# Light experts of a mixture layer: f32 products side by side on raw weights instead of products with split weights

## The chip, the cores and the metric

The kernel runs on one core of one Trainium2 chip. The metric is the device time of one execution in microseconds (us), lower is better. PE is TensorE (products), DVE is VectorE, ACT is ScalarE, POOL is GpSimd, and SP is the engine whose queue issues the loads of weights.

## The reference

Two layers of a diffusion backbone, 256 latent and 256 context tokens of width 1024, all in f32. Each layer modulates a normed input, projects it, runs three kinds of attention (GQA, differential, MLA), projects back and adds a gated result. Layer 0 has a dense feed-forward network, layer 1 a mixture of eight experts with the two best per token. The change concerns the mixture alone:

```python
def _moe_swiglu(h, w_router, w_in, w_out):
    logits = (h @ w_router).astype(jnp.float32)
    top_val, top_idx = lax.top_k(logits, TOP_K)          # TOP_K = 2 of N_EXPERTS = 8
    top_w = jax.nn.softmax(top_val, axis=-1)
    gates = jnp.sum(jax.nn.one_hot(top_idx, N_EXPERTS) * top_w[..., None], axis=-2)
    out = jnp.zeros_like(h)
    for e in range(N_EXPERTS):
        out = out + gates[..., e:e + 1] * _swiglu(h, w_in[e], w_out[e])
    return out
```

where `_swiglu(h, w_in, w_out)` is `(silu(gate) * up) @ w_out` with gate and up the two halves of `h @ w_in`; `w_in[e]` is 1024 x 3584 and `w_out[e]` 1792 x 1024. The result is close to an f32 computation.

## The kernel before

**Split products.** A product of full f32 precision is made of products of the rounded type f32r. An operand is split into a high part (a cast to f32r, on ACT, line 90) and a low part (the f32 value minus the high part, on DVE, line 91). Then high x high, high x low and low x high are added in PSUM: three matmuls for one.

**The experts** (`experts`, from line 1112; the last stage of the kernel). The router counts the tokens of each expert and ranks the experts by that count. The four with most tokens are "heavy" (128 slots for tokens), the four with fewest "light" (64 slots, `LIGHT`). They are worked on in the order heavy 0, light 4, heavy 1, light 5, 2, 6, 3, 7 (`order`, line 1121); names carry that rank, so `gub040mm` is a bank of gate products of rank 4, half 0, and `gub041s` a bank of up products of rank 4, half 1. `gather` (line 1172) picks the tokens of an expert with a product by a 0/1 matrix, for two heavy experts or all four light ones at once. `up(e, half)` makes half of gate and up (896 columns each, in two banks `mm` and two banks `s`) over eight loads of 128 rows of `w_in`, applies silu and multiplies, and transposes the result (`ht`). `down(e, half)` multiplies it with four loads of `w_out` (three with two blocks of 128 rows, one with one) into the two banks `pv` and `mod`. After the second half the sum is scaled by the gate, split, and scattered back to the tokens with a product by the transposed 0/1 matrix. For each expert the code calls `up` half 0, `down` half 1 of the expert before it, `up` half 1, `down` half 0; a scheduler then fixes the order on each engine, and the engines keep to it.

**A load** (`load`, line 1089) takes the next raw buffer in turn and issues one transfer on SP, which waits in order for that buffer to come free. There are five raw buffers (four of `rawp`, one of `xp`). Each load is then split into `wh` and `wl` (four buffers of each, `XW_BUFS`), by one cast on ACT and one subtraction on DVE over the whole load; the raw buffer is free when the subtraction is done.

**A light expert before.** Its 64 tokens' high and low parts stand side by side in one stationary operand of 128 columns (`xlight`), so that one product with `wh` and one with `wl` do for all: two passes instead of three (line 1202). One load of `w_in` is 8 products of 448 columns (12 for a heavy expert), one block of `w_out` 4 products of 512 columns (6 for a heavy one). The two halves of partitions are added afterwards: per bank two copies on ACT, two additions on DVE, then silu and a multiplication (lines 1236 to 1241).

**Two products at once.** `matmul(..., tile_position=(0, 64 * i))` puts a stationary operand of 64 columns into columns 64 i and up of the array, and its result into partitions 64 i and up. The kernel before uses it in the attention, line 779, with f32 operands and 64 columns, alternating between both places:

```python
for k in range(nk):
    for hi in range(2):
        nc.tensor.matmul(acc[64 * hi:64 * hi + 64, 0:256], lhsT=vs[hi][k], rhs=both[hi][:, k],
                         start=(k == 0), stop=(k == nk - 1), tile_position=(0, 64 * hi))
```

Line 336 (`gate_rows`) is a single f32 product of 512 columns with the full width of the array.

Of the kernel before, what the change touches and what calls it, by code (L numbers as in the profile page):

```python
# [9 lines left out]
F32 = mybir.dt.float32  # L10
# [7 lines left out]
P = 128  # L18
# [9 lines left out]
NE = 8  # L28
# [51 lines left out]
class Net:  # L80
# [1014 lines left out]

    def weights_in(self, w, half, k, b, parts=False):
        src = w[0][:, :, k, :, 896 * half:896 * half + 896].rearrange("p e g f -> p (e g) f")
        raw = self.load([P, 2, 896], src, f"wi{b}{half}{k}")
# [11 lines left out]
    def experts(self, l, mp, xp, block, acc, resid, first):  # L1110
# [58 lines left out]
        def gather(e0):  # L1169
            dispatched = dispatch(e0)  # L1170
            ne = H if light[e0] else 2
            if light[e0]:
                tiles = [make() for make in self.lights]
            else:
                tiles = {(e, s): xp.tile([P, KC, P], F32R, tag=f"xe{s}", name=f"xe{b}{e}{s}", bufs=2)
                         for e in (e0, e0 + 1) for s in "hl"}
            for k0 in range(0, KC, 2):
                ps = self.ps.tile([P, 512], F32, tag="tr", name=f"ga{b}{e0}{k0}")
                tmp = xp.tile([P, 512], F32, tag="xtmp", name=f"xt{b}{e0}{k0}")
                for u in range(2):  # L1180
# [17 lines left out]
            for u in range(ne):  # L1198
                if light[e0]:
                    xe[e0 + u] = [tiles[k // 4][:, k % 4, u].rearrange("p a s -> p (a s)") for k in range(KC)]  # L1200
                else:
                    xe[e0 + u] = [(tiles[e0 + u, "h"][:, k], tiles[e0 + u, "l"][:, k]) for k in range(KC)]
# [9 lines left out]
        def up(e, half):  # L1212
            banks = [[self.ps.tile([P, 512], F32, tag=tag, name=f"gu{b}{e}{half}{tag}{j}") for j in range(2)] for tag in ("mm", "s")]
            w = weights(e)
            for k in range(KC):
                if first and e == half == 0 and k < XW_BUFS:
                    wh, wl = self.early.pop(k)
                else:
                    wh, wl = self.weights_in(w, half, k, f"{b}{e}")
                passes = products(xe[e][k], wh, wl)  # L1220
                for n, (lhs, rhs) in enumerate(passes):
                    for gu in range(2):
                        for j in range(2):
                            nc.tensor.matmul(banks[gu][j][:, 0:448], lhsT=lhs, rhs=rhs[:, gu, 448 * j:448 * j + 448],
                                             start=(k == n == 0), stop=(k == KC - 1 and n == len(passes) - 1))
            hn = xp.tile([P, 896], F32, tag="hn", name=f"hn{b}{e}{half}")
            if light[e]:
                nc.gpsimd.memset(hn[LIGHT:P], 0.0)  # L1228
            for j in range(2):
                o = hn[:, 448 * j:448 * j + 448]  # L1230
                if light[e]:

                    o = o[0:LIGHT]
                    u = xp.tile([P, 512], F32, tag="xtmp", name=f"u{b}{e}{half}{j}")[0:LIGHT, 0:448]
                    g2, u2 = banks[0][j], banks[1][j]
                    nc.scalar.copy(out=o, in_=g2[LIGHT:P, 0:448])
                    nc.vector.tensor_tensor(out=o, in0=o, in1=g2[0:LIGHT, 0:448], op=ALU.add)
                    nc.scalar.copy(out=u, in_=u2[LIGHT:P, 0:448])
                    nc.vector.tensor_tensor(out=u, in0=u, in1=u2[0:LIGHT, 0:448], op=ALU.add)
                    nc.scalar.activation(out=o, in_=o, func=AF.Silu)  # L1240
# [3 lines left out]
                nc.vector.tensor_tensor(out=o, in0=o, in1=banks[1][j][:, 0:448], op=ALU.mult)  # L1244
            hh = xp.tile([P, 7, P], F32R, tag="hth", name=f"hth{b}{e}{half}", bufs=2)
            hl = None if light[e] else xp.tile([P, 7, P], F32R, tag="htl", name=f"htl{b}{e}{half}", bufs=2)
            for f0, nf in ((0, 4), (4, 3)):
# [3 lines left out]
                pv = ps[:, 0:nf * P].rearrange("p (f s) -> p f s", s=P)  # L1251
                if light[e]:
                    self.split(pv[:, :, 0:LIGHT], hh[:, f0:f0 + nf, 0:LIGHT], hh[:, f0:f0 + nf, LIGHT:P])
                else:
                    self.split(pv, hh[:, f0:f0 + nf], hl[:, f0:f0 + nf])
            hts[e, half] = [hh[:, f] if light[e] else (hh[:, f], hl[:, f]) for f in range(7)]

        def down(e, half):
# [7 lines left out]
            for f0 in range(0, 7, 2):  # L1266
                nf = min(2, 7 - f0)
                raw = self.load([P, nf, D], w[:, :, 7 * half + f0:7 * half + f0 + nf].rearrange("p e f n -> p (e f) n"),
                                f"wo{b}{e}{half}{f0}")
                wh = self.xw.tile([P, nf, D], F32R, tag="wh", name=f"woh{b}{e}{half}{f0}")  # L1270
# [5 lines left out]
                todo = [(f, n, lhs, rhs) for f, h, lo in held for n, (lhs, rhs) in enumerate(products(ht[f], h, lo))]  # L1276
# [3 lines left out]
                final = (6, len(products(ht[6], None, None)) - 1)  # L1280
                for (f, n, lhs, rhs), o in turns:
                    nc.tensor.matmul(ys[e][o], lhsT=lhs, rhs=rhs[:, 512 * o:512 * o + 512],
                                     start=(half == 0 and f == 0 and n == 0), stop=(half == 1 and (f, n) == final))
# [6 lines left out]
            for o in range(2):  # L1290
                sl = slice(512 * o, 512 * o + 512)
                if last:
                    yg = xp.tile([P, 512], F32, tag=("xtmp", "hn")[o], name=f"yg{b}{e}{o}")
                    nc.vector.scalar_tensor_tensor(out=yg, in0=ys[e][o], scalar=gsl, in1=self.gate[:, sl], op0=ALU.mult, op1=ALU.mult)
# [415 lines left out]
```

## Time and profile before

| | |
|---|---|
| median of 3 runs | 1532.55 us (1532.23 to 1544.02) |
| profiled execution | 1529.3 us, of which its span 1527.4 us |
| PE busy | 1387.7 us, 91% of the span |
| DVE busy | 1204.0 us, 79% |
| ACT busy | 832.0 us, 54% |
| POOL busy | 214.8 us, 14% |
| bytes moved | 318.66 MB, mean 209 GB/s |

The span is the time from the first to the last instruction of the profiled execution. Busy time counts an instruction from its start to its end; matmuls overlap one another, so a timeline shows their distance better than their durations do. An engine's row in a table of waits says for whom it stood still. The granted clock is a share of TensorE's full rate.

### The profile page before, as it was taken

Reading aid. Unit: us, or ns where it says so; the run is one execution under the profiler, and the core shown is the slowest. Engines: PE = TensorE matmul, PEld = TensorE weight load, DVE = VectorE, ACT = ScalarE, POOL = GpSimd, SP = SyncE. Lnnn points to the kernel's source line nnn. Section 1 sums busy time; section 2 is a strip of 40 time slices with the busy share of each in tenths; the row PEclk is TensorE's granted clock in tenths of the full one; section 3 lists DMA queues with packets and bytes.
Section 4 is the critical chain, followed back from the end, with each engine's and each line's share of the span. In section 5 each row is a group of like instructions: output and inputs, shape, how many; then the busy total and the mean of one; then the engine's idle time right before and its main releaser. Section 6 shows DMA issues by size and latency. Waiting matters only on the chain. (4 is left out here: it accounts for less than half of the span.)

```text
span 1527.4 us, 21068 instructions
## 1 busy us (share of the span) xinstructions
PE 1387.7 (91%) x7750; PEld 1114.6 (73%) x7750; DVE 1204.0 (79%) x1960; ACT 832.0 (54%) x1213; POOL 214.8 (14%) x174
## 2 busy tenths in 40 slices
PE   5999999999999999989999898798899899889874
PEld 1876755777789998979878556687777678767652
DVE  4577588776888787785679776888988989898896
ACT  2444455776342222234446673577767767766753
POOL 1001011111413333320220013000000000000041
PEclk9999999999999999999999999799999989999997
DMA  9265354223754566535335101499999989999982
GB/s 352 79 227 174 135 197 166 83 83 112 251 184 141 171 234 206 195 109 186 97 112 180 49 1 60 148 310 318 318 347 366 348 293 335 356 335 336 371 281 99
DMA packets 133991, 318.66 MB, mean 209 GB/s; under 512 B 7814, under 2 KB 49888, under 8 KB 133880
## 3 DMA queue, kind: packets, MB, share of 16 engines
q1 hardware_dynamic: 130032, 311.69, 58.5%
q10 hardware_dynamic: 3720, 5.54, 1.1%
q8 instruction: 63, 1.03, 0.3%
q14 instruction: 48, 0.39, 0.1%
q0 software_dynamic: 128, 0.01, 0.0%
HBM read 316.16 MB, written 1.05 MB: 208 GB/s over the span
## 5 line engine op out<-in xcount | busy, mean ns | idle before, releaser
L91 DVE TENSOR_TENSOR wilb<-wib,wihb 128x1792 fp32r<-128x1792 f32 (+1 forms) x140 | 266.6, 1933 | 24.8 <-ACT wihb L90 24.7
L90 ACT CAST wihb<-wib 128x1792 fp32r<-128x1792 f32 (+1 forms) x140 | 215.8, 1566 | 62.4 <-DMA wib<-in_moe_w_in_dram 38.4
L118 PE MATMUL fp<-hhf,fwl 128*128 128x256 f32 x704 | 199.7, 284 | 1.0 <-DVE fwl L91 1.0
L116 PE MATMUL fp<-hhf,fwh 128*128 128x256 f32 x704 | 200.0, 284 | 0.0
L117 PE MATMUL fp<-hlf,fwh 128*128 128x256 f32 x704 | 199.9, 284 | 0.0
L851 POOL TENSOR_TENSOR x<-x,otf 128x512 f32<-128x512 f32 x68 | 110.9, 1656 | 281.4 <-DVE otf L850 266.6
L91 DVE TENSOR_TENSOR wolb<-wob,wohb 128x2048 fp32r<-128x2048 f32 x64 | 128.2, 2018 | 16.4 <-ACT wohb L90 14.9
L116 PEld LDWEIGHTS fp<-hhf,fwh 128*128 128x128 f32 x704 | 134.0, 190 | 4.3 <-issue 2.6
L117 PEld LDWEIGHTS fp<-hlf,fwh 128*128 128x128 f32 x704 | 134.2, 191 | 2.9 <-issue 1.5
L118 PEld LDWEIGHTS fp<-hhf,fwl 128*128 128x128 f32 x704 | 134.0, 190 | 2.9 <-DVE fwl L91 1.5
L90 ACT CAST fwh<-fi 128x1024 fp32r<-128x1024 f32 x64 | 66.2, 1050 | 102.0 <-PE yf L118 64.9
L90 ACT CAST wohb<-wob 128x2048 fp32r<-128x2048 f32 x64 | 107.3, 1694 | 23.5 <-DMA wob<-in_moe_w_out_dram 14.3
L91 DVE TENSOR_TENSOR fwl<-fi,fwh 128x1024 fp32r<-128x1024 f32 x64 | 88.8, 1396 | 36.5 <-ACT fwh L90 36.4
L738 ACT ACTIVATE p<-s,st 128x512 f32<-128x512 f32 (+1 forms) x120 | 73.8, 618 | 25.0 <-DVE st L733 20.0
L733 DVE TENSOR_REDUCE st<-s 128x1 f32<-128x512 f32 (+1 forms) x100 | 67.8, 685 | 17.9 <-PE s L118 15.3
L1228 POOL MEMSET hnb<- 64x896 f32 x8 | 6.7, 843 | 483.8 <-PE htb L1250 483.8
L273 DVE SCALAR_TENSOR_TENSOR macc<-wm,sc,macc 128x512 f32<-128x512 f32 x84 | 73.6, 887 | 0.4
L116 PE MATMUL yf<-foh,fhh 128*128 128x512 f32 x176 | 71.9, 408 | 0.0
L118 PE MATMUL yf<-foh,fhl 128*128 128x512 f32 x176 | 70.3, 401 | 0.0
L117 PE MATMUL yf<-fol,fhh 128*128 128x512 f32 x176 | 69.8, 397 | 0.0
L91 DVE TENSOR_TENSOR fol<-fo,foh 128x1024 fp32r<-128x1024 f32 x32 | 39.0, 1222 | 25.6 <-ACT foh L90 25.5
L90 ACT CAST foh<-fo 128x1024 fp32r<-128x1024 f32 x32 | 33.5, 1049 | 45.9 <-PE fp L117 43.1
(832 smaller groups left out, 3537.4 us busy)
## 6 DMA issues: line engine op xcount, KB each, us to landing
wib<-in_moe_w_in_dram SPq DMA_DIRECT2D x128, 896.0 KB, 6.7
wm<-in_w_mod_dram SPq DMA_DIRECT2D x48, 1024.0 KB, 5.3
wob<-in_moe_w_out_dram SPq DMA_DIRECT2D x48, 1024.0 KB, 7.8
fi<-in_ffn_w_in_dram SPq DMA_DIRECT2D x64, 512.0 KB, 5.0
fo<-in_ffn_w_out_dram SPq DMA_DIRECT2D x16, 1024.0 KB, 5.2
wi<-in_w_in_dram SPq DMA_DIRECT2D x15, 1024.0 KB, 6.1
wo<-in_w_out_dram SPq DMA_DIRECT2D x12, 1024.0 KB, 5.2
wob<-in_moe_w_out_dram SPq DMA_DIRECT2D x16, 512.0 KB, 6.8
```

Of the source, the lines that this page charges most:

```text
L90: nc.scalar.copy(out=hi, in_=raw)
L91: return nc.vector.tensor_tensor(out=lo, in0=raw, in1=hi.bitcast(F32), op=ALU.subtract)
L116: t.matmul(out, lhsT=ah, rhs=bh, start=first, stop=False)
L117: t.matmul(out, lhsT=ah, rhs=bl, start=False, stop=False)
L118: t.matmul(out, lhsT=al, rhs=bh, start=False, stop=last)
L273: nc.vector.scalar_tensor_tensor(out=acc[:, s], in0=raw[:, j], scalar=c, in1=acc[:, s], op0=ALU.mult, op1=ALU.add)
L733: nc.vector.tensor_reduce(out=st[:, 0:per], in_=s.rearrange("p (u k) -> p u k", u=per), axis=AX.X, op=ALU.max, negate=True)
L738: nc.scalar.activation(out=p[:, o_], in_=s[:, o_], func=AF.Exp, bias=st[:, u:u + 1], scale=1.0, accum_out=total)
L851: (self.nc.vector if soon else self.nc.gpsimd).tensor_tensor(out=x, in0=x, in1=t, op=ALU.add)
L1228: nc.gpsimd.memset(hn[LIGHT:P], 0.0)
```

## The change

Light experts no longer split their weights nor their tokens. `gather` writes their tokens as f32 straight into one tile `xlight` (where the high parts of a former layer's input lay); the tile of the low parts becomes a raw buffer. `up` multiplies the f32 tokens (64 columns) with the raw load: the gate product in place 0, with its result in partitions 0 to 63, the up product in place 1, with its result in partitions 64 to 127. Silu reads the former and writes partitions 64 to 127, where DVE multiplies with the latter. The transposes then take 64 rows, into one bank and with one copy. `down` does the two halves of the output columns side by side in the same way, so that its sums stand in partitions 0 to 63 of one bank and 64 to 127 of the other, and scaling and scattering work on those. There are eight raw buffers (four of `rawp`, three of `xp`, one of `hp`) and three of split weights in place of four. Heavy experts are computed as before.

```diff
     def gather(e0):
...
             if light[e0]:
-                tiles = [make() for make in self.lights]
+                tiles = self.light_tokens()
...
-                tmp = xp.tile([P, 512], F32, tag="xtmp", name=f"xt{b}{e0}{k0}")
+                tmp = tiles[:, k0:k0 + 2].rearrange("p k e s -> p (k e s)") if light[e0] else \
+                    xp.tile([P, 512], F32, tag="xtmp", name=f"xt{b}{e0}{k0}")
...
+                if light[e0]:
+                    continue
                 tv = tmp.rearrange("p (k e s) -> p k e s", k=2, e=ne)
-                if light[e0]:
-                    t = tiles[k0 // 4][:, k0 % 4:k0 % 4 + 2]
-                    nc.vector.tensor_copy(t[:, :, :, 0], tv)
-                    nc.vector.tensor_tensor(out=t[:, :, :, 1], in0=tv, in1=t[:, :, :, 0].bitcast(F32), op=ALU.subtract)
-                    continue
...
-        def products(x, wh, wl):
-
-            return ((x[0], wh), (x[0], wl), (x[1], wh)) if isinstance(x, tuple) else ((x, wh), (x, wl))
+        def aside(out, lhs, rhs, u, start, stop):
+
+            nc.tensor.matmul(out[LIGHT * u:LIGHT * u + LIGHT], lhsT=lhs, rhs=rhs, start=start, stop=stop,
+                             tile_position=(0, LIGHT * u))
...
     def up(e, half):
...
             for k in range(KC):
+                if light[e]:
+                    raw = self.load([P, 2, 896], self.columns(w, half, k), f"wi{b}{e}{half}{k}")
+                    for j in range(2):
+                        for gu in range(2):
+                            aside(banks[gu][j][:, 0:448], xe[e][k], raw[:, gu, 448 * j:448 * j + 448], gu, k == 0, k == KC - 1)
+                    continue
...
                 if light[e]:
 
-                    o = o[0:LIGHT]
-                    u = xp.tile([P, 512], F32, tag="xtmp", name=f"u{b}{e}{half}{j}")[0:LIGHT, 0:448]
-                    g2, u2 = banks[0][j], banks[1][j]
-                    nc.scalar.copy(out=o, in_=g2[LIGHT:P, 0:448])
-                    nc.vector.tensor_tensor(out=o, in0=o, in1=g2[0:LIGHT, 0:448], op=ALU.add)
-                    nc.scalar.copy(out=u, in_=u2[LIGHT:P, 0:448])
-                    nc.vector.tensor_tensor(out=u, in0=u, in1=u2[0:LIGHT, 0:448], op=ALU.add)
-                    nc.scalar.activation(out=o, in_=o, func=AF.Silu)
-                    nc.vector.tensor_tensor(out=o, in0=o, in1=u, op=ALU.mult)
+                    o = o[LIGHT:P]
+                    nc.scalar.activation(out=o, in_=banks[0][j][0:LIGHT, 0:448], func=AF.Silu)
+                    nc.vector.tensor_tensor(out=o, in0=o, in1=banks[1][j][LIGHT:P, 0:448], op=ALU.mult)
                     continue
...
     def down(e, half):
...
+                if light[e]:
+                    for f in range(f0, f0 + nf):
+                        for o in range(2):
+                            aside(ys[e][o], ht[f], raw[:, f - f0, 512 * o:512 * o + 512], o, half == f == 0, half == 1 and f == 6)
+                    continue
...
+            rows = [slice(LIGHT * o, LIGHT * o + LIGHT) if light[e] else slice(0, P) for o in range(2)]
...
-                    self.raws = [(self.rawp, "raw")] * RAW_BUFS + [(xp, "raw")]
...
+                    self.raws = [(self.rawp, "raw")] * RAW_BUFS + [(self.limits(xp, {"raw": 3}), "raw"), (hp, "hl"), (self.limits(xp, {"raw": 3}), "raw"), (self.limits(xp, {"raw": 3}), "raw")]
+                    self.light_tokens = lambda: hp.tile([P, KC, NE // 2, LIGHT], F32, tag="hh", name="xlight")
...
-XW_BUFS = 4
+XW_BUFS = 3
```

How the order changes, at three places. On PE, where half 0 of the first light expert (rank 4) begins, the kernel before has (mm and s are the banks of gate and up, `wihb`/`wilb` the split weights):

```order
L1224 MATMUL gub040mm_10669<-wihb_10685,xlight_10543 128x448
L1224 MATMUL gub040mm_10670<-wihb_10685,xlight_10543 128x448
L1224 MATMUL gub040s_10671<-wihb_10685,xlight_10543 128x448
L1224 MATMUL gub040s_10672<-wihb_10685,xlight_10543 128x448
L1224 MATMUL gub040mm_10669<-wilb_10686,xlight_10543 128x448
L1184 MATMUL gab_10559<-dispb_10539,xnh_10005 128x256
L1184 MATMUL gab_10559<-dispb_10539,xnl_10007 128x256
```

and the changed kernel at the same place (`wib` is the raw load):

```order
L1207 MATMUL gub040mm_10650<-wib_10664,xlight 64x448
L1207 MATMUL gub040s_10652<-wib_10664,xlight 64x448
L1207 MATMUL gub040mm_10651<-wib_10664,xlight 64x448
L1207 MATMUL gub040s_10653<-wib_10664,xlight 64x448
L1207 MATMUL gub040mm_10650<-wib_10670,xlight 64x448
L1207 MATMUL gub040s_10652<-wib_10670,xlight 64x448
```

Eight products per load became four, gate and up alternate, and they read the raw load. In all there are 368 such products (line 1207), in 49 runs between other products.

On DVE, between the multiplication of heavy expert 0 (`gub001s`) and that of the light expert 4, the kernel before ends with these rows (`wolb` and `wilb` are subtractions for weights, `xlight` those for tokens):

```order
L1191 CAST xlight_10544<-xtb_10574 128x8x64
L1192 TENSOR_TENSOR xlight_10544<-xtb_10574,xlight_10544 128x8x64
L91 TENSOR_TENSOR wilb_10770<-wib_10767,wihb_10769 128x1792
L91 TENSOR_TENSOR wilb_10784<-wib_10781,wihb_10783 128x1792
L1191 CAST xlight_10544<-xtb_10588 128x8x64
L91 TENSOR_TENSOR wolb_10828<-wob_10825,wohb_10827 128x2048
L1192 TENSOR_TENSOR xlight_10544<-xtb_10588,xlight_10544 128x8x64
L91 TENSOR_TENSOR wolb_10846<-wob_10843,wohb_10845 128x2048
L91 TENSOR_TENSOR wolb_10864<-wob_10861,wohb_10863 128x2048
L1237 TENSOR_TENSOR hnb_10795<-hnb_10795,gub040mm_10669 64x448
L1239 TENSOR_TENSOR ub_10797<-ub_10797,gub040s_10671 64x448
```

and the changed kernel has, from the multiplication of heavy expert 0 on:

```order
L1243 TENSOR_TENSOR hnb_10513<-hnb_10513,gub001s_10367 128x448
L1243 TENSOR_TENSOR hnb_10513<-hnb_10513,gub001s_10368 128x448
L91 TENSOR_TENSOR wolb_10623<-wob_10620,wohb_10622 128x2048
L91 TENSOR_TENSOR htlb_10519<-htb_10520,hthb_10518 128x512
L91 TENSOR_TENSOR htlb_10519<-htb_10527,hthb_10518 128x384
L91 TENSOR_TENSOR wolb_10641<-wob_10638,wohb_10640 128x1024
L91 TENSOR_TENSOR wolb_10730<-wob_10727,wohb_10729 128x2048
L91 TENSOR_TENSOR wolb_10748<-wob_10745,wohb_10747 128x2048
L1240 TENSOR_TENSOR hnb_10712<-hnb_10712,gub040s_10652 64x448
L1240 TENSOR_TENSOR hnb_10712<-hnb_10712,gub040s_10653 64x448
```

The eight subtractions for loads of the light half and those for its tokens are gone; what stands between are the heavy expert's own.

On SP, the loads of `down` half 1 of heavy expert 0, with what each waits for (DMAHW are the transfer queues), in the kernel before:

```order
L1093 DMA wob_10825<-in_moe_w_out_dram 128x2x1024 [waits DMAHW1_49,DVE_49]
L1093 DMA wob_10843<-in_moe_w_out_dram 128x2x1024 [waits DMAHW2_49,DVE_49]
L1093 DMA wob_10861<-in_moe_w_out_dram 128x2x1024 [waits DMAHW3_49,DVE_49]
L1093 DMA wob_10879<-in_moe_w_out_dram 128x1024 [waits DMAHW4_49,DVE_49]
L1093 ISA
```

and in the changed one:

```order
L1093 DMA wob_10727<-in_moe_w_out_dram 128x2x1024 [waits DMAHW6_49,PE_49]
L1093 DMA wob_10745<-in_moe_w_out_dram 128x2x1024 [waits DMAHW7_49,PE_49]
L1093 DMA wob_10763<-in_moe_w_out_dram 128x2x1024 [waits DMAHW0_49,PE_49]
L1093 DMA wob_10781<-in_moe_w_out_dram 128x1024 [waits DMAHW1_49,PE_49]
L1093 ISA
```

Their buffers held light loads before, which a subtraction freed; now PE's reading frees them.

## Rows read from the trace of the kernel before

**Rows 1.** Windows of the expert stage: busy time of each engine, clock, transfers.
```profile
core 0: us, PE busy (x) PEld busy (x) DVE busy (x) ACT busy (x) POOL busy (x), PEclk, DMA share, GB/s
1019.87:1150.44 130.57, 118.16 (x572) 98.64 (x571) 118.25 (x93) 96.35 (x87) 1.69 (x2) 1.00 0.93 331
1150.44:1284.12 133.68, 120.80 (x544) 99.16 (x543) 118.68 (x101) 95.14 (x85) 1.68 (x2) 0.95 0.90 327
1284.12:1412.12 128.00, 115.02 (x513) 93.92 (x512) 114.03 (x84) 92.62 (x77) 1.69 (x2) 0.97 0.95 347
978.00:1019.87 41.87, 40.65 (x203) 35.63 (x203) 35.82 (x52) 29.48 (x27) 0.00 (x0) 0.97 0.85 288
1412.12:1500.00 87.88, 71.00 (x297) 55.81 (x296) 79.86 (x56) 58.89 (x53) 16.43 (x6) 0.94 0.86 318
```
**Rows 2.** SP's waits, 1019.87 to 1412.12: total us, times, longest us.
```profile
SPq L1093 <- DVE wilb L91: 161.2, 85, 5.9
SPq L1093 <- DVE wolb L91: 70.7, 29, 4.7
SPq L1093 <- DVE hnb L1237: 14.4, 6, 3.0
```
**Rows 3.** Windows with the transfer queue full, and just after; columns as in rows 1.
```profile
1170.00:1186.00 16.00, 12.13 (x51) 9.02 (x50) 13.13 (x9) 12.17 (x10) 0.00 (x0) 0.97 1.03 411
1186.00:1200.00 14.00, 14.00 (x62) 11.43 (x61) 13.19 (x13) 10.90 (x13) 0.84 (x1) 0.92 0.88 323
```
**Rows 4.** Groups of DVE and ACT, 1019.87 to 1412.12: busy us, mean ns | idle before.
```profile
L91 DVE TENSOR_TENSOR wilb<-wib,wihb 128x1792 fp32r<-128x1792 f32 x96 | 191.4, 2021 | 18.8 <-ACT wihb L90 18.7
L91 DVE TENSOR_TENSOR wolb<-wob,wohb 128x2048 fp32r<-128x2048 f32 (+1 forms) x48 | 96.4, 2019 | 12.2 <-ACT wohb L90 10.7 <-PE gub050mm L1224 0.7 <-PE gub060mm L1224 0.7
...
L90 ACT CAST wihb<-wib 128x1792 fp32r<-128x1792 f32 x96 | 160.8, 1696 | 46.4 <-DMA wib<-in_moe_w_in_dram 30.9 <-PE yb00mod L1282 4.0 <-PE gub031s L1224 3.2
L90 ACT CAST wohb<-wob 128x2048 fp32r<-128x2048 f32 (+1 forms) x49 | 82.6, 1699 | 20.8 <-DMA wob<-in_moe_w_out_dram 11.6 <-PE gub021s L1224 2.8 <-PE gub040s L1224 2.4
```
**Rows 5.** Timeline of PE, heavy expert 1: start us, us, product, records.
```profile
1104.47 0.57 PE L1224 MATMUL gub010s<-wilb,xeb01h 128*128 128x448 f32 x2
...
1106.12 0.57 PE L1224 MATMUL gub010s<-wihb,xeb01h 128*128 128x448 f32 x2
```
**Rows 6.** Timeline of PE, light expert 4, products of 512 columns.
```profile
1091.34 0.40 PE L1282 MATMUL yb04pv<-wohb,hthb 128*128 128x512 f32 x1
...
1092.50 0.40 PE L1282 MATMUL yb04mod<-wohb,hthb 128*128 128x512 f32 x1
```
**Rows 7.** One f32 product of 512 columns: timeline, and all of line 336.
```profile
988.69 1.02 PE L336 MATMUL gr<-gp,consts 128*128 128x512 f32 x2
...
L336 PE MATMUL gr<-gp,consts x8: 590/592/696, 846.1 to 990.7; 128*128 128x512 f32 x8
```
**Rows 8.** Timeline of PE around line 779, attention of layer 1.
```profile
918.38 0.40 PE L118 MATMUL s<-mk11h,ringhh 96*128 96x512 f32 x1
918.71 1.94 PE L779 MATMUL pv<-pt,dkv 128*64 128x256 f32 x14
920.58 0.66 PE L760 MATMUL tp<-consts,p 128*128 128x128 f32 x4
```
**Rows 9.** Transfer issues of the expert weights: count, KB each, us to landing.
```profile
wib<-in_moe_w_in_dram SPq DMA_DIRECT2D x128, 896.0 KB, 6.7
...
wob<-in_moe_w_out_dram SPq DMA_DIRECT2D x48, 1024.0 KB, 7.8
...
wob<-in_moe_w_out_dram SPq DMA_DIRECT2D x16, 512.0 KB, 6.8
```
**Rows 10.** Timeline of the end, DVE and ACT, last light expert.
```profile
1484.11 0.53 ACT L1236 COPY hnb<-gub071mm 64x448 f32<-64x448 f32 x1 [8.39 <-PE gub071mm L1224]
...
1494.68 0.61 DVE L1241 TENSOR_TENSOR hnb<-hnb,ub 64x448 f32<-64x448 f32 x1
...
1506.08 0.75 DVE L1294 SCALAR_TENSOR_TENSOR ygb<-yb07pv,gslb,gate 128x512 f32<-128x512 f32 x1 [0.86 <-PE yb07pv L1282]
```

More of the change, by code (lines that the diff above doesn't have):

```diff
@@ L1094, in load, with columns @@
         return raw
+    @staticmethod
+    def columns(w, half, k):
+        return w[0][:, :, k, :, 896 * half:896 * half + 896].rearrange("p e g f -> p (e g) f")
     def weights_in(self, w, half, k, b, parts=False):
-        src = w[0][:, :, k, :, 896 * half:896 * half + 896].rearrange("p e g f -> p (e g) f")
-        raw = self.load([P, 2, 896], src, f"wi{b}{half}{k}")
+        raw = self.load([P, 2, 896], self.columns(w, half, k), f"wi{b}{half}{k}")
         wh = self.xw.tile([P, 2, 896], F32R, tag="wh", name=f"wih{b}{half}{k}")
@@ L1244, in up @@
                 nc.vector.tensor_tensor(out=o, in0=o, in1=banks[1][j][:, 0:448], op=ALU.mult)
+            if light[e]:
+                ht = xp.tile([P, 7, LIGHT], F32, tag="hth", name=f"ht{b}{e}{half}", bufs=2)
+                ps = self.ps.tile([P, 512], F32, tag="tr", name=f"ht{b}{e}{half}")
+                for f in range(7):
+                    nc.tensor.transpose(ps[:, f * LIGHT:(f + 1) * LIGHT], hn[LIGHT:P, f * P:(f + 1) * P], self.ident[LIGHT:P, LIGHT:P])
+                nc.scalar.copy(out=ht.rearrange("p f s -> p (f s)"), in_=ps[:, 0:7 * LIGHT])
+                hts[e, half] = [ht[:, f] for f in range(7)]
+                return
             hh = xp.tile([P, 7, P], F32R, tag="hth", name=f"hth{b}{e}{half}", bufs=2)
-            hl = None if light[e] else xp.tile([P, 7, P], F32R, tag="htl", name=f"htl{b}{e}{half}", bufs=2)
+            hl = xp.tile([P, 7, P], F32R, tag="htl", name=f"htl{b}{e}{half}", bufs=2)
             for f0, nf in ((0, 4), (4, 3)):
@@ L1250, in up @@
                     nc.tensor.transpose(ps[:, f * P:(f + 1) * P], hn[:, (f0 + f) * P:(f0 + f + 1) * P], self.ident)
[L1251 to L1256, printed above, removed]
+                self.split(ps[:, 0:nf * P].rearrange("p (f s) -> p f s", s=P), hh[:, f0:f0 + nf], hl[:, f0:f0 + nf])
+            hts[e, half] = [(hh[:, f], hl[:, f]) for f in range(7)]
         def down(e, half):
@@ L1275, in down @@
                     continue
-                todo = [(f, n, lhs, rhs) for f, h, lo in held for n, (lhs, rhs) in enumerate(products(ht[f], h, lo))]
+                todo = [(f, n, lhs, rhs) for f, h, lo in held
+                        for n, (lhs, rhs) in enumerate(((ht[f][0], h), (ht[f][0], lo), (ht[f][1], h)))]
                 turns = [(t, o) for o in range(2) for t in todo] if last and half and f0 == 6 else \
                     [(t, o) for t in todo for o in range(2)]
-                final = (6, len(products(ht[6], None, None)) - 1)
                 for (f, n, lhs, rhs), o in turns:
                     nc.tensor.matmul(ys[e][o], lhsT=lhs, rhs=rhs[:, 512 * o:512 * o + 512],
-                                     start=(half == 0 and f == 0 and n == 0), stop=(half == 1 and (f, n) == final))
+                                     start=(half == 0 and f == 0 and n == 0), stop=(half == 1 and (f, n) == (6, 2)))
                 held = []
@@ L1289, in down @@
             dt, gsl = dts.pop(e)
-            for o in range(2):
+            rows = [slice(LIGHT * o, LIGHT * o + LIGHT) if light[e] else slice(0, P) for o in range(2)]
+            for o, r in enumerate(rows):
                 sl = slice(512 * o, 512 * o + 512)
@@ L1301, in down @@
                     nc.gpsimd.tensor_tensor(out=resid[i], in0=resid[i], in1=acc[i], op=ALU.add)
-            for o in range(2):
+            for o, r in enumerate(rows):
                 for i in range(2):
```

30 lines of the change are left out of this document (13 added, 17 removed).

## The prediction

> **What bounds the kernel now.** I read the windows view over the expert stage first. Weights begin to multiply at 978 us; from the first light expert on, one heavy and one light expert together ("a pair") take 130.57, 133.68 and 128.00 us [rows 1], 130.75 on average, and the two pieces at the ends add up to one more pair, so the stage is 522 us, four pairs of 130.5. In each of the three stretches PE is busy about 118 us, DVE 114 to 119 and the DMA engines nine tenths of the time, at 327 to 347 GB/s: three resources close to full and none of them quite.
>
> Then the waits of the queue that issues the loads: over 392 us of that stage SP stood 161.2 us for DVE's subtraction on input weights and 70.7 us for the one on output weights, and less for other DVE work queued among them, such as the additions of a light product's halves (14.4 us, the largest of a dozen small rows) [rows 2]. A raw buffer comes free only when DVE has subtracted, so DVE's place in its queue sets when the next transfer may start. That the wires are not the limit is in the windows again: where five buffers happened to be full of requests, the engines moved 411 GB/s for 16 us; in the 14 us after it 323 [rows 3].
>
> DVE's time is mostly the split: 96 subtractions of 2021 ns and 48 of 2019 ns in three pairs; ACT's are 96 casts of 1696 ns and 49 of 1699 ns [rows 4]. Per expert that is 16 x 2.021 + 8 x 2.019 = 48.5 us on DVE and 40.7 us on ACT.
>
> **The change, part by part.** *Splits removed.* Four light experts lose their casts and subtractions: 48.5 us of DVE and 40.7 us of ACT per pair, and DVE falls from 118 to about 65 us a pair with the shorter evacuation (each pair loses also eight additions of a light product's two halves, which stand in the same queue). No light load waits for DVE any more: the order above shows SP waiting for PE there.
>
> *Light products.* Before, one load of 896 KB is 8 products of 448 columns. Eight of them start between 1104.47 and 1106.12 us, 0.206 us apart [rows 5]; the products of 512 columns stand 0.233 us apart (five steps from 1091.34 to 1092.50) [rows 6]. A light expert is 16 x 8 x 0.206 + 14 x 4 x 0.233 = 39.4 us; a heavy one, with 12 and 6, 39.6 + 19.6 = 59.2 us. After, it is f32 products with 64 tokens as the stationary side. An f32 product leaves two records: the gate row, one product of 512 columns, shows 2 records in 1.02 us, of 592 ns each [rows 7], so the second starts 0.43 us after the first: an f32 product costs nearly four times one of the present kind. It pays only if two of them run at once. Line 779, in the attention, does just that: 64 columns wide, f32, two places side by side. Its eight products of 256 columns (16 records, 14 of them recorded) take 1.94 us in all [rows 8]; less the last one's 0.38 us that is 1.56 us for seven rounds, 0.223 us each, two records per round. One after the other the 16 records would need some 3.5 us. Scaled by columns, a round is 0.39 us at 448 and 0.446 us at 512, a pair of products 0.78 and 0.89. A light expert: 16 x 2 x 0.78 + 14 x 0.89 = 37.4 us, 2.0 less than now. The transposes of the light h are half as wide: another 0.7.
>
> *Switches.* The order holds 49 runs of paired products among others, so 98 switches, 24.5 a pair. Before line 779 the ordinary step of 0.23 is 0.33 us (918.38 to 918.71) [rows 8]: 0.1 us more. That is 2.4 us a pair. The Trainium skill, TensorEngine Tiling (Array Packing), Key Properties, has a rule against the change: a change of the tiling mode drains the engine. If a drain were a whole record of line 779, 0.38 us, the 98 would cost 37 us instead of 10, and the time would come out 27 us later than by the row. I stay with the row.
>
> *Raw buffers 5 to 8, split buffers 4 to 3.* The gain has no row of its own; its bounds come from transfers. A pair is 2 x 21504 KB = 44.04 MB [rows 9]. At 411 GB/s this takes 107.2 us, the lower bound. With the present 327 to 347 it is 127 to 135, so at worst nothing is gained, or a little lost. A light load keeps its buffer until PE has read it, where a split used to free it, but PE uses a light load (1.56 us) faster than it lands (2.24 us at 411 GB/s). The third split buffer less costs a heavy load this: cast 1.70, subtraction 2.02, products 12 x 0.206 = 2.47, some 0.2 us for handing over, 6.4 us in all; with three buffers one is ready every 2.1 us, and PE takes one in 2.47. It is hidden as long as ACT and DVE are not held up by more than about a microsecond, and DVE now has half its time free. If that cover is gone, see below.
>
> *The sum for a pair.* PE: 118.0 busy, less 2.0, less 0.7, plus 2.4: 117.7 us. Transfers: 107.2 or more. DVE: 65. So PE is late next. Its busy time includes half-rate stretches (granted clock 1.00, 0.95, 0.97 [rows 1], that is some 3.5 us) and drawn-out matmuls around each pause, so true work is less, nearer 110; against that some of today's 12.8 us of idle time will stay, because transfers with 107 us are almost as full and the two run through eight buffers. I let these cancel and take 117.7 us, between 107.2 and 130.5: 4 x (130.5 - 117.7) = 51 us gained.
>
> *End.* After the last input product, h of the last light expert needs ACT and DVE six steps per half, queued among splits: 1484.11 to 1495.3 us; its output sums are complete at 1506.08 [rows 10]. Now it is one activation and one multiplication per half, some 2 us, and no split before the last products; but the last eight loads still have to land. I take 6 us off. The loads ahead of the first product are gated by memory that the router frees, and PE's start at 978 us by the router: nothing for the start.
>
> Sum: 57 us off. The profiled execution took 1529.3 us (span 1527.4): 1472 us; the median of the three runs, 1532.55, stands 3.25 above the profiled one, so **1475 us**. This machine tells about 1% of this kernel from no change, 15 us.
>
> **The rivals.** *PE's pauses vanish and the transfers bound the stage.* A pair then takes 109 us, near the 107.2: 86 us gained, 92 with the end, 1441 us. For it: 411 GB/s is sustained whenever requests are queued, and light stretches, now heavy on DVE, become cheap. Against it: heavy experts still need 59 us of products plus transposes and gathers, and PE idles at each change of phase today.
>
> *Transfers get no faster.* If 347 GB/s, the best whole stretch, is a limit, a pair is 126.9 us: 14 us gained, 20 with the end, 1512 us. Against it stands the 411. The Trainium skill, SBUF — State Buffer, Summary: rules for kernel authors, tells one to estimate reads of HBM at about 358 GB/s; by that a pair would take 123 us and the kernel come out near 1497 us. The trace's 411 speaks against that figure as a limit here.
>
> *Three split buffers starve the heavy experts.* If ACT or DVE regularly hold a split up, a heavy load goes from 2.47 to some 2.9 us, 24 loads by 0.4 us, 10 us a pair: 127.7 us, 11 us gained, 17 with the end, 1515 us. For it: ACT and DVE work their queues in order, and evacuations stand among the casts. Against: DVE loses half its work.
>
> *Slower: the two products don't run side by side.* Here they write two different banks, while those of line 779 share one, and gathers and transposes are put between some of them. If the second product waits for the first, a light expert costs 74.8 us, a pair 117.7 + 37.4 = 155: 98 us more for four, less 6, so 1625 us. It decides from 12.8 us more per pair on: when a pair of products takes a third longer than two rounds, say 0.52 us a round for 448 columns. Against it: line 779 is the same form and width.
>
> **How the numbers follow.** Forecast 0.58; transfers bound 0.17; transfers no faster 0.09; starved 0.09; slower 0.07. Alone the forecast reaches from 1455 to 1495. The range of 8 in 10 takes in the transfer-bound case on one side and the two small gains on the other: 1437 to 1517 us. Faster by over 1% (under 1517): 0.58 + 0.17 and some 0.10 of the two small-gain cases, 0.85; within 1% 0.08; slower by over 1% 0.07.
>
> **What would show it.** Right: in the changed profile the light products start in pairs, rounds of 0.38 to 0.40 us at 448 columns; no cast and no subtraction of a light load; a pair of experts takes 112 to 122 us and transfers run at 360 to 395 GB/s; SP waits for PE as well as DVE. The pairing is wrong if rounds of 448 columns come one after the other for the two halves; the switches are mis-sized if each run of light products begins 0.4 us late; the third split buffer is the trouble if PE waits for subtractions in heavy stretches more than now. If the DMA rate stays near 345 with free buffers, the transfer bound was wrong; if PE's clock falls to 1.2 GHz in light stretches, where it waits for transfers, the light products were mis-sized.

## The result, and the profile after

The changed kernel takes 1495.14 us (median of 4 runs, 1484.03 to 1502.28), the kernel before 1534.78 us (4 runs, 1532.23 to 1544.02): a ratio of 0.9725, 95% interval [0.9651, 0.9798]. It is faster by 39.6 us, where 57 were forecast. The profiled execution took 1495.41 us (span 1493.5), 33.9 less than that of before.

First the windows view of the changed kernel: three pairs between the same transfer issues as in [rows 1], then the whole stage, from its first product to the output sums of the last light expert; behind the length stand busy time of PE, PEld, DVE, ACT and POOL with counts, the granted clock, the DMA share and GB/s.

```profile
1022.28:1143.56 121.28, 118.92 (x562) 77.41 (x561) 63.34 (x49) 54.97 (x53) 0.00 (x0) 0.97 0.95 360
1143.56:1273.91 130.35, 122.62 (x550) 77.57 (x549) 67.73 (x65) 54.06 (x52) 0.00 (x0) 0.96 0.91 332
1273.91:1391.95 118.04, 112.92 (x506) 71.17 (x505) 63.09 (x48) 49.40 (x43) 0.00 (x0) 0.97 0.99 381
...
985.10:1473.10 488.00, 467.25 (x2141) 299.82 (x2140) 256.19 (x236) 207.41 (x192) 9.39 (x4) 0.97 0.93 346
```

A pair takes 123.2 us on average (130.75 before); the second gained least (130.35 against 133.68). DVE is down to 63 to 68 us, as forecast. PE is busy 118.2 us a pair, as before, and idle 5.1 instead of 12.8. Its clock is no better: over the stage 0.97 stands for some 15 us lost at half rate (0.03 x 488; the last digit is worth 2.5 us), and so it was before. The same view of the kernel before, over the same stage, first product to last output sums:

```profile
977.75:1506.86 529.11, 471.20 (x2141) 386.79 (x2140) 472.88 (x390) 374.79 (x327) 21.49 (x12) 0.97 0.90 324
```

The stage is 41.1 us shorter. It began 7.3 us later in this execution (985.10 against 977.75), behind layers that the change does not touch, and that is why the whole gained only 33.9. That start is chance: in the fourteen executions profiled for this document it lies anywhere from 976.80 to 988.53 us.

The timeline of PE in a light expert: start, duration in us, product; 448 columns, then 512.

```profile
1050.12 0.54 PE L1207 MATMUL gub040mm<-wib,xlight 128*64 128x448 f32 x1
1050.12 0.54 PE L1207 MATMUL gub040s<-wib,xlight 128*64 128x448 f32 x1
1050.49 0.54 PE L1207 MATMUL gub040mm<-wib,xlight 128*64 128x448 f32 x1
1050.50 0.54 PE L1207 MATMUL gub040s<-wib,xlight 128*64 128x448 f32 x1
...
1093.73 0.59 PE L1207 MATMUL yb04pv<-wob,htb 128*64 128x512 f32 x1
1093.73 0.59 PE L1207 MATMUL yb04mod<-wob,htb 128*64 128x512 f32 x1
1094.16 0.59 PE L1207 MATMUL yb04pv<-wob,htb 128*64 128x512 f32 x1
```

Two records start together, in two different banks, and the next two 0.376 us later (0.43 at 512 columns): the products run side by side. And where a run of them begins and ends (timeline of PE):

```profile
1071.99 0.39 PE L1290 MATMUL yb00pv<-wohb,htlb 128*128 128x512 f32 x1
1072.22 0.40 PE L1290 MATMUL yb00mod<-wohb,htlb 128*128 128x512 f32 x1
1072.55 0.97 PE L1207 MATMUL gub041mm<-wib,xlight 128*64 128x448 f32 x2
...
1076.10 0.54 PE L1207 MATMUL gub041s<-wib,xlight 128*64 128x448 f32 x1
1076.58 0.50 PE L1317 MATMUL scb<-yhb,dispTb 128*128 128x512 f32 x1
1076.91 0.40 PE L1318 MATMUL scb<-ylb,dispTb 128*128 128x512 f32 x1
1077.24 0.59 PE L1207 MATMUL gub041s<-wib,xlight 128*64 128x448 f32 x1
1077.67 0.54 PE L1207 MATMUL gub041s<-wib,xlight 128*64 128x448 f32 x1
```

The step into a run is 0.33 us against 0.23, the step out 0.48 against 0.376: 0.1 us across each switch. But the step behind it is longer too: 0.43 us for the first round of the run (1077.24 to 1077.67), 0.33 for the first full product after one (1076.58 to 1076.91). Both ends together cost some 0.35 us a run, 0.17 a switch; the medians over the stage's 49 runs are the same.

The waits of SP over the same length as in [rows 2], 392 us from the first of the three pairs on (1022 to 1414 us): total, times, longest.

```profile
SPq L1093 <- DVE wilb L91: 96.9, 49, 5.0
SPq L1093 <- DVE wolb L91: 55.1, 27, 4.4
SPq L1093 <- PE htb L1257: 20.4, 3, 6.8
SPq L1093 <- PE gub041s L1207: 17.4, 7, 7.9
SPq L1093 <- PE gub051s L1207: 15.1, 7, 8.4
```

Against [rows 2] the waits for DVE fell by a third, and new ones for PE came in: a load waits until PE has reached the light load that sits in its buffer. PE's own waits (1015 to 1480 us):

```profile
PE htb L1248 <- DVE hnb L1240: 3.1, 7, 1.0
PE scb L1317 <- DVE macc L1326: 2.7, 3, 0.9
PE gub020mm L1231 <- ACT wihb L90: 2.2, 1, 2.2
PE yb03pv L1290 <- DVE wolb L91: 2.1, 2, 1.6
PE yb01pv L1290 <- DVE wolb L91: 2.1, 2, 1.6
```

(`scb` is the scattering product, `macc` the sum that it is added to.) But for the first row, a light expert's transposes that wait for its own multiplication, they lie where one expert follows another. What such a pause does to the clock is in windows of 5 us (PE fell idle at 1129 us, waiting for the additions of a light expert's output):

```profile
1075.00:1080.00 5.00, 5.00 (x24) 1.98 (x22) 2.68 (x4) 0.59 (x1) 0.00 (x0) 1.00 1.03 407
...
1125.00:1130.00 5.00, 4.09 (x16) 1.23 (x12) 2.29 (x4) 2.95 (x3) 0.00 (x0) 1.00 1.03 406
1130.00:1135.00 5.00, 4.96 (x12) 3.04 (x13) 4.72 (x5) 3.27 (x3) 0.00 (x0) 0.59 1.03 407
1135.00:1140.00 5.00, 5.00 (x20) 4.47 (x20) 4.30 (x3) 1.91 (x2) 0.00 (x0) 0.73 1.02 400
```

After 0.9 us of idle time the clock falls from 2.4 to 1.2 GHz for 6.8 of the next 10 us ((1 - 0.59) x 2 x 5 and (1 - 0.73) x 2 x 5). All of this while the transfers run at 400 GB/s and more; over 45 us on end:

```profile
1095.00:1140.00 45.00, 44.04 (x186) 29.76 (x183) 29.83 (x22) 22.41 (x19) 0.00 (x0) 0.92 1.03 407
```

### The profile page after: what moved, and what is told of

The parts are those of the page before. It is cut to its first block, busy times and chain, and to the rows that moved or that the text cites. A ratio compares the mean times of both kernels' runs of the same rounds, so it can differ in the third digit from the quotient of the medians.

```text
span 1493.5 us, 20561 instructions
## 1 busy us (share of the span) xinstructions
PE 1391.4 (93%) x7750; PEld 1032.5 (69%) x7750; DVE 986.9 (66%) x1805; ACT 663.1 (44%) x1074; POOL 202.8 (14%) x166
## 5 line engine op out<-in xcount | busy, mean ns | idle before, releaser
L91 DVE TENSOR_TENSOR wilb<-wib,wihb 128x1792 fp32r<-128x1792 f32 (+1 forms) x73 | 131.6, 1815 | 32.0 <-ACT wihb L90 31.9
L90 ACT CAST wihb<-wib 128x1792 fp32r<-128x1792 f32 (+1 forms) x73 | 108.3, 1505 | 45.4 <-PE gub031s L1231 7.7
L91 DVE TENSOR_TENSOR wolb<-wob,wohb 128x2048 fp32r<-128x2048 f32 (+1 forms) x32 | 64.0, 2023 | 29.4 <-ACT wohb L90 29.4
L1310 POOL TENSOR_TENSOR macc<-macc,gate 128x1024 f32<-128x1024 f32 x2 | 4.7, 2360 | 475.5 <-DVE macc L1326 475.5
L90 ACT CAST wohb<-wob 128x2048 fp32r<-128x2048 f32 (+1 forms) x32 | 53.6, 1696 | 22.5 <-DMA wob<-in_moe_w_out_dram 11.8
L760 PE MATMUL tp<-consts,p 128*128 128x128 f32 x320 | 51.6, 286 | 5.5 <-ACT p L738 4.7
```

The lines of the kernel that those rows point to most:

```text
L90: nc.scalar.copy(out=hi, in_=raw)
L91: return nc.vector.tensor_tensor(out=lo, in0=raw, in1=hi.bitcast(F32), op=ALU.subtract)
L760: nc.tensor.transpose(tp[:, (k * per + u) * P:(k * per + u + 1) * P], p[:, u * nkeys + k * P:u * nkeys + (k + 1) * P], self.ident)
L1310: nc.gpsimd.tensor_tensor(out=acc[i], in0=acc[i], in1=self.gate, op=ALU.mult)
```

## The experiments

Two questions: which part of the change carries the gain, and why 17 us of the forecast are missing. Stage lengths are from first product to last output sums, as above, from one execution each; PE's idle time is the stage less its busy time; the half-rate loss is (1 - clock) x stage, good to some 2.5 us. Each ratio is to executions of the kernel before that ran beside that kernel (their median was 1531 to 1536 us).

| kernel | raw, split buffers | median us | ratio to before, 95% | stage us | PE idle | half-rate loss |
|---|---|---|---|---|---|---|
| before | 5, 4 | 1534.78 | | 529.1 | 57.9 | 16 |
| changed | 8, 3 | 1495.14 | 0.9725 [0.9651, 0.9798] | 488.0 | 20.8 | 15 |
| b7x3 | 7, 3, no f32 | 1528.45 | 0.9976 [0.9947, 1.0004] | 523.5 | 52.1 | 16 |
| r5x4 | 5, 4 | 1541.02 | 1.0054 [1.0026, 1.0082] | 534.1 | 53.8 | 27 |
| r6x4 | 6, 4 | 1522.51 | 0.9921 [0.9893, 0.9948] | 516.0 | 34.9 | 31 |
| r6x3 | 6, 3 | 1519.65 | 0.9901 [0.9865, 0.9937] | 519.7 | 37.5 | 31 |
| r7x3 | 7, 3 | 1502.39 | 0.9787 [0.9728, 0.9846] | 501.6 | 24.9 | 25 |
| r10x2 | 10, 2 | 1514.96 | 0.984 [0.9784, 0.9896] | 509.3 | 34.1 | 15 |
| twoprod | 8, 3 | 1439.48 | 0.9371 [0.9317, 0.9425] | 438.6 | 38.4 | 22 |
| fewload | 8, 3 | 1473.40 | 0.9586 [0.9533, 0.9638] | 467.2 | 6.9 | 9 |
| seq | 8, 3 | 1594.93 | 1.0411 [1.0379, 1.0444] | 591.1 | 3.3 | 0 |
| whole | 8, 3 | 1491.31 | 0.975 [0.9719, 0.9781] | 491.8 | 22.6 | 15 |
| early2 | 8, 3 | 1501.39 | 0.9793 [0.9767, 0.9818] | 495.7 | 21.8 | 25 |
| early3 | 8, 3 | 1479.38 | 0.9636 [0.9611, 0.9662] | 478.7 | 14.9 | 10 |

**The buffers alone (b7x3)**: the kernel before with

```diff
-self.raws = [(self.rawp, "raw")] * RAW_BUFS + [(xp, "raw")]
+self.raws = [(self.rawp, "raw")] * RAW_BUFS + [(self.limits(xp, {"raw": 3}), "raw")] * 3
-XW_BUFS = 4
+XW_BUFS = 3
```

> The kernel of before with seven raw buffers and three split ones, light experts split as before: the buffers alone. If DVE's subtractions set the pace there (114 to 119 us of work in a pair of 131), more raw buffers gain nothing and one split buffer less costs a little: 1530 to 1545 us. If the queueing of transfers carries the gain, 1505 to 1515 us.

Measured 1528.45 us, no difference that can be told. Its pair without a gather (output sums of expert 5 to those of expert 6) has DVE busy 114.5 of 125.2 us: with the splits still there, buffers are not what it lacks. (One split buffer fewer came with the two raw ones more; that its loss hides a small gain was not tried.)

**The f32 products alone (r5x4)**: the changed kernel with

```diff
-self.raws = [(self.rawp, "raw")] * RAW_BUFS + [(self.limits(xp, {"raw": 3}), "raw"), (hp, "hl"), ...
+self.raws = [(self.rawp, "raw")] * RAW_BUFS + [(self.limits(xp, {"raw": 1}), "raw")]
-XW_BUFS = 3
+XW_BUFS = 4
```

> The f32 products of the light experts alone, with the five raw and four split buffers of before. If the f32 products carry the gain (no subtraction holds a raw buffer in light stretches), most of the 40 us stays: 1490 to 1505 us. If the eight raw buffers carry it, it falls back to 1520 us or more.

Measured 1541.02 us: a little slower than before. Nearly half of DVE's work in the stage is gone (255 us instead of 473) and nothing is gained; so neither the products alone nor, up to seven, the buffers alone gain anything. The windows of 5 us around the first light expert show why:

```profile
1075.00:1080.00 5.00, 5.00 (x19) 1.62 (x20) 2.95 (x5) 1.09 (x2) 0.00 (x0) 1.00 0.06 25
1080.00:1085.00 5.00, 5.00 (x36) 3.43 (x34) 1.21 (x3) 1.17 (x2) 0.00 (x0) 1.00 0.73 212
...
1100.00:1105.00 5.00, 2.79 (x12) 0.77 (x12) 0.00 (x0) 0.37 (x1) 0.00 (x0) 1.00 1.03 409
1105.00:1110.00 5.00, 2.66 (x9) 2.10 (x10) 3.42 (x2) 3.85 (x3) 0.00 (x0) 0.88 1.03 406
1110.00:1115.00 5.00, 5.00 (x21) 4.51 (x21) 4.52 (x3) 3.84 (x3) 0.00 (x0) 0.78 1.03 407
```

From 1075 to 1080 us PE is fully busy and the transfers stand still (25 GB/s): the five buffers hold light loads that PE has not reached (SP's waits for PE in the second half of this expert's input products come to 18.1 us, the longest 8.7). Twenty-five us later the transfers run at 409 GB/s, PE is idle nearly half the time for want of weights, and its clock falls behind that. With eight buffers the first of these windows, shown above, moved 407 GB/s.

**Six and seven raw buffers (r6x3, r6x4, r7x3)**: in r6x3

```diff
-self.raws = [(self.rawp, "raw")] * RAW_BUFS + [(self.limits(xp, {"raw": 3}), "raw"), (hp, "hl"), ...
+self.raws = [(self.rawp, "raw")] * RAW_BUFS + [(self.limits(xp, {"raw": 1}), "raw"), (hp, "hl")]
```

r6x4 has XW_BUFS = 4 besides; r7x3 has two buffers in xp beside that in hp.

> The changed kernel with six raw buffers instead of eight, three split buffers as in the change. If the raw buffers carry the gain by keeping the transfers queued, two fewer give back part of it: a pair of experts goes from 123 us to some 126, and the time to about 1507 us. If PE's work and its pauses at the change from one expert to the next set the time, it stays within 0.5% of the changed kernel, 1490 to 1503 us.

> Six raw and four split buffers, to be read beside the kernel with six and three. If three split buffers hold up the heavy experts, where PE still stands idle 4 us and runs part of the time at half rate, the fourth takes some 3 to 5 us off each of the four pairs: 1475 to 1485 us. If the pauses come from the order of the work on ACT and DVE at a change of expert, it makes no difference: the time of the kernel with six and three, within 0.5%.

> The changed kernel with seven raw buffers. Six gave 1520 us, eight 1495. If light loads that PE has not yet reached hold the buffers and stop the transfers, each buffer counts alike: about 1507 us. If eight is merely beyond a threshold and seven is not, 1517 to 1522 us.

With six, 1519.65 us, more lost than either theory gave; with seven 1502.39. So the price is graded: 17 us for the seventh buffer, 7 for the eighth by the medians. The seventh is clear of noise; for the eighth the two intervals overlap. A fourth split buffer beside six raw ones changes nothing (the two intervals overlap). Of the 31.7 us by which the stage of r6x3 is longer, 16.7 are idle time of PE and some 16 the half rate behind it: taken together, the added pauses are paid about twice.

**Ten raw, two split (r10x2)**: five buffers in xp beside that in hp, XW_BUFS = 2.

> Ten raw buffers, two split ones (the same memory as in the change). With two split buffers a heavy load takes (1.70 + 2.02 + 2.47 + 0.2) / 2 = 3.2 us instead of 2.47 of products, 24 times 0.73 = 17 us in a pair: 1550 us if nothing is given back. If the depth of raw buffers goes on paying 12 us apiece as between six and eight, it gives back 25 us: some 1530 us. If two split buffers are enough, 1470 to 1480 us.

Measured 1514.96 us, none of the three. Two split buffers cost some 20 us net, far less than 70. How much of a larger loss the two extra raw buffers gave back was not tried.

**Less work for PE (twoprod)**:

```diff
-for n, (lhs, rhs) in enumerate(((xh, wh), (xh, wl), (xl, wh))):
+for n, (lhs, rhs) in enumerate(((xh, wh), (xh, wl))):
...
-        for n, (lhs, rhs) in enumerate(((ht[f][0], h), (ht[f][0], lo), (ht[f][1], h)))]
+        for n, (lhs, rhs) in enumerate(((ht[f][0], h), (ht[f][0], lo)))]
```

> The changed kernel without the third product of the heavy experts (the one with the low part of the activations): that part of the computation is left out. PE has 16 x 4 x 0.206 + 14 x 2 x 0.233 = 19.7 us less to do in a pair, transfers as many as before. If PE's work alone sets the pair, 79 us less: about 1416 us. If the transfers are next at 107 to 110 us a pair (now 122), 48 to 60 us less: 1435 to 1447 us. If transfers stopped by full buffers set it, less than half of the 79: 1460 us or more.

Measured 1439.48 us, the transfers' case. The windows view, whole stage and the pair from expert 5's output sums to expert 6's:

```profile
976.80:1415.41 438.61, 400.17 (x1773) 234.94 (x1772) 252.85 (x236) 206.30 (x193) 9.40 (x4) 0.95 0.99 384
1217.34:1325.40 108.06, 98.62 (x424) 57.39 (x424) 62.70 (x49) 49.80 (x44) 0.00 (x0) 0.94 1.00 387
```

With 20 us less of products the transfers hardly ever stop (share 0.99 of the stage), and the pair takes 108 us, where 107.2 had been worked out for them.

**Fewer transfers (fewload)**:

```diff
-    raw = self.load([P, 2, 896], self.columns(w, half, k), f"wi{b}{e}{half}{k}")
+    if k % 2 == 0:
+        raw = self.load([P, 2, 896], self.columns(w, half, k), f"wi{b}{e}{half}{k}")
```

> The changed kernel with every second input load of the light experts left out, its products taken from the load before it (so that part of the computation is not what it should be, with as many products as before). A pair has 40 loads instead of 48, 90 us of transfers at 411 GB/s. If PE's pauses and its half-rate stretches in the changed kernel (20 us and 14 us over the stage) come from transfers that start too late, they go: a pair falls from 122 to about 113 us, the time to some 1460 us. If they come from the order of the work of ACT and DVE where one expert follows another, they stay: 1485 to 1497 us.

Measured 1473.40 us, between the two. PE's idle time falls from 20.8 to 6.9 us and the clock rises to 0.98: two thirds of the pauses were weights that came late. I read this as a kernel held by PE and by the transfers in turn, where eight buffers do not quite carry one over the other's slow part; whether the loads left out helped by the wires or by the buffers that they no longer held, the run does not tell.

**Not side by side (seq)**:

```diff
-nc.tensor.matmul(out[LIGHT * u:LIGHT * u + LIGHT], lhsT=lhs, rhs=rhs, start=start, stop=stop,
-                 tile_position=(0, LIGHT * u))
+nc.tensor.matmul(out[0:LIGHT], lhsT=lhs, rhs=rhs, start=start, stop=stop,
+                 tile_position=(0, 0))
```

with the evacuations reading rows 0 to 63 of both banks.

> The changed kernel with both products of a light expert in the same 64 columns of the array, so that they cannot run side by side; the same products otherwise. If pairs of f32 products really overlap (rounds of 0.376 us with both in it), a light expert takes 72 us of PE instead of 36, a pair 113 + 36 = 149 or a little more instead of 122: 1600 to 1630 us. If PE was waiting for transfers in light stretches anyhow, half of that: 1540 to 1560 us.

Measured 1594.93 us, slower than before by 4%: pairing is worth 100 us. Its stage in the windows view:

```profile
984.41:1575.50 591.09, 587.76 (x2141) 338.38 (x2140) 256.60 (x235) 208.52 (x193) 9.35 (x4) 1.00 0.80 285
```

PE has hardly a pause, and the clock is 1.00 over the stage. Its f32 products of 448 columns now start one by one, 0.376 us apart.

**The order at a change of expert (whole, early2, early3).** whole puts both output halves of a heavy expert one after the other:

```diff
-    if i:
+    if i and not (first and not light[order[i - 1]]):
         down(order[i - 1], 1)
...
     down(e, 0)
+    if first and not light[e]:
+        down(e, 1)
```

> The changed kernel with both output halves of a heavy expert one after the other, so that 20 light loads follow each other in the queue where at most 12 did. If the number of light loads in a row against eight buffers is what counts, PE outruns the transfers for longer: 1503 to 1520 us. If the handing over from heavy to light and back is what costs, one of them less in each pair gains: 1480 to 1490 us.

Measured 1491.31 us, as the changed kernel. Both theories missed, the second by little: PE now waits 2.2 to 2.5 us for the first input load of heavy experts 1, 2 and 3 in place of the output loads. The number of light loads in a row was too coarse a rule.

early2 and early3 fetch and split the first two or three output loads of a heavy expert's second half ahead of the next light expert's input loads (fetch is the load and split of down, moved into a function; early3 has range(0, 6, 2)):

```diff
+    if light[e]:
+        for f0 in range(0, 4, 2):
+            ready[order[i - 1], 1, f0] = fetch(order[i - 1], 1, f0)
     up(e, 0)
...
-    raw = self.load([P, nf, D], w[...], f"wo{b}{e}{half}{f0}")
+    got = ready.pop((e, half, f0), None) or fetch(e, half, f0)
```

> The changed kernel with the first two output loads of a heavy expert's second half, and their splits, set ahead of the next light expert's eight input loads; same products, same buffers. If raw buffers that hold light loads PE has not reached are what makes the heavy expert's last output loads late (PE stands 8 us for them in three places of the changed kernel, with a half-rate stretch of 3.4 to 6.8 us behind each), the waits go and part of the half-rate with them: 1478 to 1487 us. If the wires or PE's work alone set the pair, nothing moves: 1490 to 1500 us.

Measured 1501.39 us: no gain. ACT's timeline tells why (the last bracket is the idle time before and what ended it):

```profile
1182.25 0.54 ACT L1252 ACTIVATE hnb<-gub050mm 64x448 f32<-64x448 f32 x1 [17.55 <-PE gub050s L1207]
1183.00 0.54 ACT L1252 ACTIVATE hnb<-gub050mm 64x448 f32<-64x448 f32 x1 [0.22 <-PE gub050s L1207]
1183.56 1.90 ACT L90 CAST wohb<-wob 128x2048 fp32r<-128x2048 f32 x1
```

ACT stood 17.55 us at an activation that needs the light expert's last product, with the cast of the third output load queued behind it. PE then waited for that cast and its subtraction, as in the changed kernel:

```profile
PE yb03pv L1300 <- DVE wolb L91: 2.3, 3, 1.6
...
PE yb03pv L1300 <- ACT wohb L90: 0.8, 1, 0.8
```

> As the kernel with two output loads set ahead, but three. There the third load was in its buffer when ACT turned to two activations of the light expert that wait for PE, and its cast stood behind them; with three ahead, three casts stand before them. If this order of ACT is what makes PE wait there (9.4 us at the output products of the heavy experts over the stage, half-rate stretches behind), the waits fall to some 3 us and the time to 1483 to 1492 us. If PE only changes what it waits for, because the light loads now come three later on the same wires, 1497 to 1507 us, as with two ahead.

Measured 1479.38 us, a little better than expected. The same rows of PE's waits shrink to one:

```profile
PE yb03pv L1300 <- DVE wolb L91: 1.3, 3, 0.5
```

and the stage is

```profile
979.66:1458.37 478.71, 463.85 (x2141) 296.56 (x2140) 256.41 (x236) 207.47 (x193) 9.31 (x4) 0.98 0.94 352
```

5.9 us less idle time and 3.4 less busy time than in the changed kernel (half-rate loss 10 instead of 15, each good to 2.5). All five of its runs (1477.89 to 1483.56) lie below the fastest of the changed kernel's four (1484.03): by the runs it beats both kernels, though against the changed one the two intervals just touch.

## Why the prediction was right, and where its size was off

The direction and the main mechanism were right (DVE's splits held the buffers, PE comes next), the size was not: 57 us forecast, 39.6 measured between the medians, 33.9 between the profiled executions. That is inside the wide range, which took in two rivals, but at the very edge of what the forecast alone was to reach (1455 to 1495). Of its own signs two failed: a pair took 123.2 us, not 112 to 122, and of the three rates (360, 332, 381 GB/s) the second lies below 360.

- *Splits removed.* Forecast 65 us of DVE in a pair; 63.3, 67.7 and 63.1. Right.
- *Light products.* Forecast rounds of 0.39 and 0.446 us, 37.4 us per light expert. Measured 0.376 and 0.43: 64 x 0.376 + 28 x 0.43 = 36.1. Right, and the same in two banks as in one. The rival (not side by side) was priced at 1625 us, 155 a pair; seq took 1595, with 146.9 us of PE's work a pair (a quarter of its stage) and hardly any of it at half rate. Less the second 36.1 that makes some 111 us by my estimate, the "nearer 110" of the prediction for true work.
- *Switches.* Forecast 0.1 us each, from the one step into line 779. The steps across show that, but the steps behind them are longer too: 0.17 us a switch, 17 us for the 49 runs where 10 were forecast. The Trainium skill, TensorEngine Tiling (Array Packing), Key Properties, says that a change of tiling mode drains the engine; here it shows as 0.17 us a switch, not as the whole record of 0.38 that the prediction tried.
- *PE's busy time.* Forecast 117.7 us in a pair; 118.92, 122.62 and 112.92, mean 118.2. Right, in part by luck: the switches cost 1.9 us a pair more than forecast, the light products 1.3 less.
- *The step that failed* is "I let these cancel and take 117.7 us": the pair was set equal to PE's busy time, half-rate and drawn-out time to be won back, remaining idle time lost, both alike. The half-rate time stayed (0.97, 0.96, 0.97), and 5.1 us of idle time a pair came on top: 123.2 us. They do not cancel but add up: a quarter of the stage, 122.0 us, is some 111 us of true work, 5.2 of idle time and 6 of drawn-out work, 3.7 of it half rate. The three middle pairs gained 22.6 us (392.25 to 369.67) instead of 38.4. The two ends, forecast at one pair and 6 us, 18.8 together, gained the other 18.5 of the stage's 41.1. The start, costed at nothing, lost 7.3 in this execution: 57.2 - 15.8 - 0.3 - 7.3 = 33.8.
- *Behind it* lies a cost that I put at nothing: "PE uses a light load (1.56 us) faster than it lands". True, but the buffer is held from the landing until PE *reaches* the load, past a heavy expert's products, where a split used to move it on to one of the split buffers. r5x4 shows the price, 8 us more than before, and the raw buffers from five to eight, given no term, turn that into the gain. Eight leave the 5.1 us; fewload, with a third of it left (6.9 us of 20.8 over the stage), and early3 show that much of it can go.
- *Transfers bound the stage* (1441 us) did not come, but twoprod shows its floor at 108 us a pair.
- *Transfers no faster* fell as a limit: the changed kernel moved 407 GB/s over 45 us on end, and twoprod 384 over its stage. The Trainium skill, SBUF — State Buffer, Summary: rules for kernel authors, gives some 358 GB/s for an estimate; twoprod's 384 speaks against that figure as a limit. The Trainium skill, HBM Reference, Specifications (TRN2), says that a core streaming alone gets well above that share, and these runs on one core agree. Yet the prediction's sum by the 358, 123 us a pair and 1497 us in all, comes nearer to the measured 123.2 and 1495 than the forecast does. That is chance: the three pairs moved 357 GB/s on average, but with less work for PE the same transfers ran at 384 over the whole stage.
- *Three split buffers starve* fell as a matter of number: with six raw ones a fourth split buffer changes nothing (r6x4 equals r6x3; beside eight it was not tried). Its reason, evacuations that stand among the casts, was real: early2 shows a cast held up behind two of them, and early3 what setting the casts ahead gives back.

## What to carry to other kernels

When an engine drops out of a chain, ask how long the buffer that it used to empty is now held: until the next reader reaches it in its own order, not for as long as it reads. Removing the work and adding the buffers was worth 2.7%, the first alone -0.5%, the second alone (seven buffers) nothing that could be told. And where an engine idles behind an in-order queue, look for the instruction at its head: setting three casts before an activation that waits for PE gained about another per cent.

## What the runs showed of the hardware

A pause of PE can cost twice its length: from eight raw buffers to six, idle time and half-rate loss rose alike (20.8 to 37.5 us and 15 to 31), and 0.9 us of idle time was followed by windows at 0.59 and 0.73 of the clock. It is no fixed price: the kernel before had 57.9 us of idle time and lost only 16 at half rate. With hardly a pause (seq), 147 us of work a pair ran at a clock of 1.00. Two f32 products 64 columns wide ran side by side into two different banks, both starting within 0.01 us and the next two 0.376 us later. A run of such products among full ones cost some 0.35 us more than its steps add up to, nearly half of it in the step behind each switch.
